# Two edits in a two-layer attention trunk: one gate projection moved in the fill order, and a bias moved from TensorE to GpSimd and VectorE

## The chip, the cores and the metric

One Trainium2 chip, one core. The metric is the device time of one execution in microseconds (us). TensorE (PE) multiplies matrices, VectorE (DVE), ScalarE (ACT) and GpSimd (POOL) do the rest, SyncE (SP) issues the DMAs. A matmul shows twice in the trace, as a weight load (PEld) and as the pass of the moving columns (PE).

## The reference, cut to what matters

Two layers on 1024 tokens of width 1024, in float32. Layer 1 holds an attention that keeps the 256 best keys of each query (DSA, "a") and a sliding-window attention ("b"); layer 2 holds a compressed, selected and windowed attention (NSA, "c") and a latent attention ("d"). Each output is multiplied by silu of a gate projection ("z").

```python
y = rms_norm(x, norm_g) @ w_in              # layer 1: qa ka va qi ki wi za qb kb vb zb
score = sum_h wi * relu(qi @ ki.T)          # index scores
idx = top_k(score, 256)                     # a search of 32 steps here, giving a mask
oa = attention(qa, ka, va, masked by idx)
ob = sliding_window_attention(qb, kb, vb)
x = x + concat(oa * silu(za), ob * silu(zb)) @ w_out

# layer 2, one part of it: the compression of keys (n=0) and values (n=1)
def nsa_compress(z, pe, w1, w2):            # z: 63 overlapping blocks of 32 tokens
    flat = (blocks + pe).reshape(..., 32 * 64)
    return silu(flat @ w1) @ w2             # w1: 2048 x 128
```

`flat @ w1` is worked out as `blocks @ w1 + pe @ w1`. The second term is the position bias, 128 numbers for each n.

## The kernel before, in words

Tokens are cut into 8 tiles of 128. All projections of a layer are cut into chunks of up to 280 columns. For a chunk, `w_quarter` loads the weights (line 472), splits them into a high part on ACT (line 476) and a low part on POOL (line 477); `fill_gen` then makes 24 matmuls for each token tile (lines 520 to 522, into one of two `pp` banks of PSUM), and the chunk's `post` empties the bank.

* A query chunk (`qa0`, `qa1`, `qb0`, ...) empties through `pair_in`: two ACT copies for each tile (lines 452 and 454, the second into the one `sq` buffer). Two tiles make a pair, which goes through `head_chain` (POOL and DVE) to a transpose (line 392) and to one of three `qs` buffers (lines 396 and 399). The chain holds one of four `nz` buffers until the transpose.
* A gate chunk (`z0`, `z1`, `z2`) empties through `gate_post`: one ACT tanh (line 610), one DVE product (line 611), one DMA out. `z2` has 270 columns, `qa0` and `qa1` have 256 each.

`FAO` is the order in which the chunks of layer 1 are issued as fill beside the other work, by planned costs. A query chunk is held back (`q_gate`) while all three `qs` buffers are in use. The search for the 256 best keys (`topk`) runs beside this: a step counts on ACT (line 904, three token tiles) and on DVE (line 908, three tiles), compares (line 919) and moves the candidate (line 921). When the second half of the search ends, lines 960 to 966 build the masks, one for each of the token tiles 2 to 7; each mask uses one of the three `pt` buffers, which the attention of "b" and "a" also uses for its scores (lines 680 and 683). The blocks of "a" from tile 2 on wait for their masks.

The framework under the kernel orders the instructions of each engine: what is issued earlier in the program has priority, what is ready earlier by its own estimate may go in front. On the chip each engine then runs its own list in that order.

In layer 2, `compress` is posted when the chunk `kc` ends, and runs in small steps between the fill's matmuls of the chunk `kw`. For n = 0 and then for n = 1 it loads `pe` and `w2`, makes the bias by 16 matmuls of one column each (line 1265), multiplies the blocks by the same 16 weight tiles (line 1276), and goes on with tanh, `w2` and the key or value form. The first-layer compression weights `w1` (1 MB for each n) lie in slots of a five-slot pool; the trace calls them `w`. The load of the second `w1` (line 1224) is issued when a slot of that pool comes free.

Of the kernel before, what the change touches and what calls it, by code (L numbers as in the profile page):

```python
# [10 lines left out]
F32 = mybir.dt.float32  # L11
# [7 lines left out]
OP = mybir.AluOpType  # L19
AX = mybir.AxisListType  # L20
PSUM = bass.MemoryType.PSUM

P = 128
# [29 lines left out]
BR = 0.8  # L53
AR = 1.2

FAO = 'ki qi kb qb0 z0 z1 qb1 ka qa0 z2 qa1'
FOO = 'ks kc kw qc0 zc0 zc1 cq qc1 zd0 zd1 ck'
SR = 0.6
GDA = [2, 3, 7], [4, 5, 6]
# [11 lines left out]
PTB = 3  # L71
# [113 lines left out]
def trunk(ctx: ExitStack, tc: tile.TileContext, A, out):  # L185
    nc = tc.nc
    V, S, G, T = nc.vector, nc.scalar, nc.gpsimd, nc.tensor
# [4 lines left out]
    wk = ctx.enter_context(tc.tile_pool(name="wk", bufs=2))  # L192
# [25 lines left out]
    half = cst.tile([P, 16], F32, name="half")  # L218
# [140 lines left out]
    def tps():  # L359
        return psT.tile([P, 4, P], F32, name="psT")  # L360
# [679 lines left out]
    z0 = zlo + 206  # L1040
    z1 = z0 + 274
# [34 lines left out]
    def seq(*gens):  # L1076
        for g in gens:
# [3 lines left out]
                  qa0=c_qa[0], qa1=c_qa[1])  # L1081
    FA = fill_gen([chunks[n] for n in FAO.split()])
    L.pump(FA, ("qi", 2))
# [4 lines left out]
    for c in tk:  # L1088
        m += c
        L.tick()  # L1090
        while f < TR * m and c is not None:
            c = next(FA)
# [161 lines left out]
    def compress():  # L1254
        for n in range(2):
            w1 = B["w1"][n]
            zT = B["zT"][n]
            pe = cp.tile([P, 16], F32, name="pe")
            nc.sync.dma_start(pe, A["c_cmp_pe"][0, n].rearrange("(a b) d -> (b d) a", b=2))
            w2 = cp.tile([P, 64], F32, name="w2")  # L1260
            nc.sync.dma_start(w2, A["c_cmp_w2"][0, n])
            yield from L.take_in("psT", PTC)
            ph = tps().rearrange("p a n -> p (a n)")
            for a in range(16):
                T.matmul(ph[:, 0:1], w1[:, a], pe[:, a:a + 1], start=a == 0, stop=a == 15)
            bias = cp.tile([P, 2], F32, name="bias", bufs=2)
            V.tensor_copy(bias[:, 0:1], ph[:, 0:1])
            L.give("psT")
            V.tensor_scalar(bias[:, 1:2], bias[:, 0:1], 0.5, None, op0=OP.mult)
            yield  # L1270
# [4 lines left out]
            for a in range(16):  # L1275
                T.matmul(p2[:, :, 0:NCMP], w1[:, a], zT[:, :, 2 * a:2 * a + 16 * (NCMP - 1) + 1:16],
                         start=a == 0, stop=a == 15)
# [196 lines left out]
    def cchunk(*a, **k):  # L1474
        return chunk(*a, src="x1T", **{"tiles": AO[1], **k})

    c_kc = cchunk(wcd, CD["kc"], CD["ks"], kc_post, pre=kc_pre,
                 post_all=lambda: L.post(compress()))
    c_ks = cchunk(wcd, CD["ks"], CD["kw"], ksq, pre=ksp)
    c_kw = cchunk(wcd, CD["kw"], CD["zc"], kw_post, pre=kwp, post_all=kw_all)  # L1480
# [387 lines left out]
```

## Time and profile before

| what | value |
|---|---|
| median of 3 runs | 1495.83 us (1494.69 to 1501.79) |
| profiled execution, its own time | 1506.33 us |
| its span, first to last instruction | 1504.5 us |
| mean granted TensorE clock in it | 0.944 |
| PE busy in the span | 1331.0 us (88%) |
| DVE, ACT, POOL busy | 1004.0, 939.7, 908.6 us |

The profiled execution is one run, with the profiler on; it lies 10.5 us above the median. Durations are read from it, differences are carried over to the median.

### The profile page before, as it was taken

To read this page: it belongs to the slowest core of one execution; us is meant where nothing else is said; L and a number is where in the kernel's file an instruction comes from. 1 tells how busy PE (TensorE), PEld (TensorE's weight loads), DVE (VectorE), ACT (ScalarE), POOL (GpSimd) and SP (SyncE) were. 2 spreads that over 40 slices of the span, in tenths; PEclk is the share of its full clock that TensorE was granted. 3 is DMA by queue.
4 is the path that set the end of the run, shared out by engine and by line. 5 is a ranking of instruction groups with operands and counts; after the bars stand their busy time and mean duration, and the time that the engine had idled before them with its cause. 6 is when DMAs were issued, how large, how long until landed. Compare 5 with 4: busy or idle time off the path is not lost. (4 is left out here: it accounts for less than half of the span.)

```text
span 1504.5 us, 33785 instructions
## 1 busy us (share of the span) xinstructions
PE 1331.0 (88%) x12132; PEld 1221.2 (81%) x12132; DVE 1004.0 (67%) x2788; ACT 939.7 (62%) x2683; POOL 908.6 (60%) x1196
## 2 busy tenths in 40 slices
PE   5998899888248999999999998899998868889998
PEld 5998888788247788999999997699996757778887
DVE  5397887787887966244225757756668889986552
ACT  5354588877658866144424677866768869866531
POOL 6798648896467486227349353365244799875440
PEclk9999999898659999999999999999999879999999
DMA  6311264322041244132311253312334414334442
GB/s 205 91 32 31 68 134 92 81 49 69 12 109 59 83 108 131 44 120 70 75 33 53 75 106 76 64 46 62 78 61 71 117 56 98 82 86 102 128 128 79
DMA packets 208936, 122.81 MB, mean 82 GB/s; under 512 B 141696, under 2 KB 193664, under 8 KB 208768
## 3 DMA queue, kind: packets, MB, share of 16 engines
q1 hardware_dynamic: 208768, 120.65, 32.0%
q8 instruction: 95, 1.56, 0.4%
q14 instruction: 73, 0.60, 0.1%
HBM read 67.65 MB, written 23.07 MB: 60 GB/s over the span
## 5 line engine op out<-in xcount | busy, mean ns | idle before, releaser
L520 PE MATMUL pp<-whi,Rh 128*128 128x256 f32 (+4 forms) x1648 | 483.2, 294 | 22.7 <-ACT sq L454 6.6
L521 PE MATMUL pp<-wlo,Rh 128*128 128x256 f32 (+4 forms) x1648 | 477.6, 290 | 1.1 <-POOL wlo L477 1.1
L522 PE MATMUL pp<-whi,Rl 128*128 128x256 f32 (+4 forms) x1648 | 478.2, 290 | 0.0
L520 PEld LDWEIGHTS pp<-whi,Rh 128*128 128x128 f32 x1648 | 319.3, 194 | 28.4 <-ACT sq L454 7.7
L521 PEld LDWEIGHTS pp<-wlo,Rh 128*128 128x128 f32 x1648 | 319.4, 194 | 3.1 <-POOL wlo L477 1.5
L522 PEld LDWEIGHTS pp<-whi,Rl 128*128 128x128 f32 x1648 | 319.4, 194 | 1.1
L689 ACT ACTIVATE pt<-pt,nm 128x256 f32<-128x256 f32 (+8 forms) x384 | 244.9, 640 | 5.5
L477 POOL TENSOR_TENSOR wlo<-wraw,whi 128x256 fp32r<-128x256 f32 (+4 forms) x208 | 163.5, 795 | 129.2 <-ACT whi L476 123.0
L711 POOL TENSOR_TENSOR hl<-pt,hl 128x512 f16<-128x512 f32 x114 | 136.9, 1203 | 110.1 <-ACT hl L710 83.6
L476 ACT ACTIVATE whi<-wraw 128x256 fp32r<-128x256 f32 (+4 forms) x208 | 83.2, 416 | 135.6 <-DMA wraw<-in_cd_w_in 48.2
L730 PE MATMUL psT<-identf,pt 128*128 128x128 f32 x800 | 144.7, 286 | 12.4 <-ACT pt L689 6.0
L733 ACT ACTIVATE hp<-psT 128x512 f16<-128x512 f32 (+3 forms) x241 | 109.0, 462 | 59.9 <-PE psT L730 55.5
L683 DVE CUSTOM_DVE_ANT_0 pt<-psS,mk 128x512 f32<-128x512 f32 (+4 forms) x208 | 107.0, 522 | 47.9 <-PE psS L680 37.1
L734 DVE TENSOR_TENSOR hp<-psT,hp 128x512 f16<-128x512 f32 (+3 forms) x241 | 123.3, 521 | 23.1 <-ACT hp L733 21.7
L303 POOL TENSOR_TENSOR rs_y<-rs_v,half 128x8 f32<-128x8 f32 (+3 forms) x102 | 122.5, 1203 | 3.9
L730 PEld LDWEIGHTS psT<-identf,pt 128*128 128x128 f32 x800 | 95.5, 144 | 26.2 <-ACT pt L689 13.7
L660 PEld LDWEIGHTS <-hp 128*128 128x128 f16 x800 | 73.4, 98 | 26.0 <-ACT hp L733 7.6
L687 ACT ACTIVATE nm<-nm 128x1 f32<-128x1 f32 (+2 forms) x208 | 42.0, 203 | 83.6 <-DVE nm L683 82.4
L663 PEld LDWEIGHTS <-hp 128*128 128x128 f16 x800 | 72.1, 98 | 23.8 <-DVE hp L734 14.7
L661 PEld LDWEIGHTS <-hp 128*128 128x128 f16 x800 | 73.7, 99 | 2.7 <-issue 1.8
L710 ACT ACTIVATE hl<-pt 128x512 f16<-128x512 f32 x114 | 71.0, 628 | 7.6 <-DMA ht<-hl 4.9
L689 ACT ACTIVATION_READ_ACCUMULATOR pt<-pt,nm 128x1 f32 x384 | 73.5, 191 | 0.0
(317 smaller groups left out, 3641.8 us busy)
## 6 DMA issues: line engine op xcount, KB each, us to landing
wraw<-in_cd_w_in SPq DMA_DIRECT2D x72, 128.0 KB, 2.1
wraw<-in_ab_w_in SPq DMA_DIRECT2D x56, 128.0 KB, 2.5
xs<-in_x SPq DMA_DIRECT2D x8, 512.0 KB, 6.0
od<-mx SPq DMA_DIRECT2D x32, 128.0 KB, 1.9
wraw<-in_ab_w_out SPq DMA_DIRECT2D x32, 128.0 KB, 2.2
x<-in_x SPq DMA_DIRECT2D x8, 512.0 KB, 4.7
mo<-od SPq DMA_DIRECT2D x16, 256.0 KB, 3.0
nz<-zdr SPq DMA_DIRECT2D x16, 256.0 KB, 3.0
```

The costliest lines, as they stand in the source:

```text
L303: G.tensor_tensor(y, v, half[:w, :n], OP.pow)
L476: S.activation(hi[:, :o], raw[:, :o], AF.Copy)
L477: G.tensor_tensor(lo[:, :o], raw[:, :o], hi[:, :o].bitcast(F32), OP.subtract)
L520: T.matmul(ps, xh, hi[:, :n], start=q == 0 and k == 0, stop=False)
L521: T.matmul(ps, xh, lo[:, :n], start=False, stop=False)
L522: T.matmul(ps, xl, hi[:, :n], start=False, stop=q == 3 and k == 1)
L683: V.tensor_tensor_reduce(pt[:, j * nk + c:j * nk + c + w], ps[:, at:at + w], mask(c, w), -1.0, first, op0=OP.add, op1=OP.min, accum_out=low)
L689: S.activation(pt[:, j * nk:(j + 1) * nk], pt[:, j * nk:(j + 1) * nk], AF.Exp, scale=-1.0, bias=nm[:, h:h + 1], accum_out=sm[:, h:h + 1])
L711: (V if way[-1] == "d" else G).tensor_tensor(hl[:, w:], pt[:, o:o + w], hl[:, :w], OP.subtract)
L730: T.transpose(pT[:, a], pt[:, o:o + P], identf)
L733: S.activation(ph, pT[:, :n], AF.Copy)
L734: V.tensor_tensor(pl, pT[:, :n], ph, OP.subtract)
```

## The change

`FAO` issues the gate chunk `z2` directly behind `ka`, in front of the query chunk `qa0`; before, it came between `qa0` and `qa1`. And `compress` makes its position bias in another way: POOL multiplies the 16 weight tiles by `pe` (two products of 128 x 1024), DVE sums each product over its 8 tiles (two reductions to 128 x 128), and PE sums over the partitions by two matmuls with a column of the constant `half` (-0.5); the factor -2 goes into the copy out of PSUM. Two more steps (`yield`) stand in the generator. The product takes a `pt` buffer, the sums an `mx` buffer.

```diff
-FAO = 'ki qi kb qb0 z0 z1 qb1 ka qa0 z2 qa1'
+FAO = 'ki qi kb qb0 z0 z1 qb1 ka z2 qa0 qa1'
@@ compress()
             w2 = cp.tile([P, 64], F32, name="w2")
             nc.sync.dma_start(w2, A["c_cmp_w2"][0, n])
+
+            u = wk.tile([P, 256], F32, name="pesum", tag="mx", bufs=3)
+            for a in range(0, 16, 8):
+                t = wk.tile([P, 1024], F32, name="pt", bufs=PTB).rearrange("p (a c) -> p a c", a=8)
+                G.tensor_tensor(t, w1[:, a:a + 8], pe[:, a:a + 8, None].to_broadcast([P, 8, P]), OP.mult)
+                V.tensor_reduce(u[:, 16 * a:16 * a + P], t.rearrange("p a c -> p c a"), AX.X, OP.add)
+                yield
             yield from L.take_in("psT", PTC)
             ph = tps().rearrange("p a n -> p (a n)")
-            for a in range(16):
-                T.matmul(ph[:, 0:1], w1[:, a], pe[:, a:a + 1], start=a == 0, stop=a == 15)
+            for a in range(2):
+                T.matmul(ph[:, 0:1], u[:, a * P:(a + 1) * P], half[:, 0:1], start=a == 0, stop=a == 1)
             bias = cp.tile([P, 2], F32, name="bias", bufs=2)
-            V.tensor_copy(bias[:, 0:1], ph[:, 0:1])
+            V.tensor_scalar(bias[:, 0:1], ph[:, 0:1], -2.0, None, op0=OP.mult)
             L.give("psT")
```

## Rows read from the trace of the kernel before

**Rows 1.** Windows: us of the stretch, then busy us of each engine, clock, DMA

```profile
450.00:600.00 150.00, 137.68 (x1608) 122.08 (x1607) 109.70 (x320) 115.70 (x302) 101.89 (x128) 0.98 0.31 93
600.00:916.00 316.00, 311.31 (x2737) 305.98 (x2736) 139.88 (x412) 143.73 (x428) 148.96 (x213) 0.97 0.27 73
```

**Rows 2.** Waits of PE between 600 and 916: the longest in total, times, longest

```profile
PE pp L520 <- DVE x L1160: 1.7, 2, 1.4
```

**Rows 3.** Timeline of PE: first matmuls of qa0, z2 and qa1, and the gap

```profile
291.49 0.58 PE L520 MATMUL pp<-whi,Rh 128*128 128x256 f32 x1 [3.75 <-DVE vla L603]
...
329.06 0.37 PE L520 MATMUL pp<-whi,Rh 128*128 128x270 f32 x1
...
360.56 0.28 PE L520 MATMUL pp<-whi,Rh 128*128 128x256 f32 x1
...
404.31 0.79 PE L680 MATMUL psS<-kb,qs 128*128 128x256 f32 x2 [22.42 <-DVE nm L683]
```

**Rows 4.** By line or tile: count, min/median/max ns, first and last start

```profile
L921 DVE SCALAR_TENSOR_TENSOR cand<-inc,less x15: 166/167/899, 318.4 to 391.9; 128x6 f32<-128x6 f32 x15
...
L921 DVE SCALAR_TENSOR_TENSOR cand<-inc,less x5: 167/167/596, 376.4 to 391.9; 128x6 f32<-128x6 f32 x5
...
L960 ACT ACTIVATE sel<-hi,K x4: 624/772/926, 301.4 to 414.3; 128x384 bf16<-128x384 int16 x1, 128x512 bf16<-128x512 int16 x1, 128x640 bf16<-128x640 int16 x1, 128x768 bf16<-128x768 int16 x1
...
L680 PEld LDWEIGHTS psS<-ka,qs x44: 186/192/338, 432.6 to 469.7; 128*128 128x128 f32 x44
```

**Rows 5.** Groups of ACT between 312.7 and 395.6: busy us, mean ns, idle before

```profile
L610 ACT ACTIVATE zst<-pp 128x270 f32<-128x270 f32 x8 | 3.1, 385 | 2.6 <-PE pp L522 2.4
L454 ACT ACTIVATE sq<-pp 128x256 f32<-128x256 f32 x8 | 3.0, 374 | 0.0
L452 ACT ACTIVATE nz<-pp 128x256 f32<-128x256 f32 x8 | 2.9, 368 | 0.7 <-PE pp L522 0.7
```

**Rows 6.** Timeline of PE's weight loads around the two biases

```profile
740.38 0.48 PEld L1239 LDWEIGHTS psT<-identf,ydup 128*128 128x128 f32 x4
740.84 4.35 PEld L1265 LDWEIGHTS psT<-pe,w 128*128 128x128 f32 x32
...
745.07 5.24 PEld L1276 LDWEIGHTS psT<-zT,w 128*128 128x128 f32 x24
750.20 0.32 PEld L520 LDWEIGHTS pp<-whi,Rh 128*128 128x128 f32 x1
...
751.11 1.61 PEld L1276 LDWEIGHTS psT<-zT,w 128*128 128x128 f32 x8
...
765.36 4.91 PEld L1265 LDWEIGHTS psT<-pe,w 128*128 128x128 f32 x32
770.14 0.33 PEld L522 LDWEIGHTS pp<-whi,Rl 128*128 128x128 f32 x1
...
771.46 5.14 PEld L1276 LDWEIGHTS psT<-zT,w 128*128 128x128 f32 x24
```

**Rows 7.** Windows around the biases, columns as in rows 1

```profile
745.00:750.00 5.00, 5.00 (x25) 5.00 (x25) 0.31 (x2) 0.72 (x2) 1.42 (x2) 0.50 0.30 47
...
760.00:765.00 5.00, 5.00 (x41) 4.94 (x39) 2.00 (x5) 1.09 (x5) 4.69 (x11) 1.00 0.02 5
...
770.00:775.00 5.00, 5.00 (x24) 4.97 (x25) 1.42 (x5) 1.17 (x5) 2.09 (x3) 0.56 0.00 0
```

**Rows 8.** Groups by shape, POOL and DVE: nearest to the new operations

```profile
L374 POOL TENSOR_TENSOR nz<-nz,rs_y 128x512 f32<-128x512 f32 x24 | 25.7, 1072 | 0.6
L1512 POOL TENSOR_TENSOR Rl<-wraw,Rh 128x512 fp32r<-128x512 f32 x16 | 22.0, 1375 | 0.3 <-ACT Rh L1511 0.3
L595 DVE TENSOR_REDUCE vs_m<-pt 128x1 f32<-128x1024 f32 x5 | 6.1, 1218 | 3.7 <-DMA pt<-in_cd_w_in 2.0 <-DMA pt<-in_ab_w_in 1.7
```

**Rows 9.** Compression weights: issues on SP (first and last start), and the landing

```profile
L1224 SPq DMA_DIRECT2D w<-in_c_cmp_w x2: 718/772/826, 717.3 to 753.2; - x2
...
DMA to landing us min/median/max: 2.2/4.2/6.6
```

## The prediction

> **What bounds the kernel now.** I read the page first: PE is busy 88% of the span, no other engine over 67%. Then windows along the whole span, to see where that average hides something. Between 600 and 916 us PE is busy 311 of 316 us [rows 1], and the waits of PE in that stretch add up to little, the longest group to 1.7 us [rows 2]: here PE alone sets the end, so a microsecond of PE work that goes is a microsecond won, and what follows starts earlier by as much. Both biases of the compression lie in that stretch. Between 450 and 600 us (attention "a") PE is busy 138 of 150 us and stands idle for 12.3 [rows 1].
>
> The other half of the change lies in front of that. In the timeline of PE, `qa0` starts at 291.49, `z2` at 329.06, `qa1` at 360.56, and at 404.31 a product of "b" begins after 22.4 us in which PE did nothing [rows 3]. The reader should see that PE waits there for no projection: the wait is on DVE, and the search for the best keys runs there, its candidate moved for the last but one time at 391.9 [rows 4]. The masks copied in from 301.4 on hold `pt` buffers until the search ends [rows 4], and the last blocks of "b" need those. So the end of the search starts the rest of layer 1; the first product of "a" follows at 432.6 [rows 4].
>
> **The moved chunk.** Nothing is added or removed: 8 tiles of 24 matmuls of `z2`, their 8 ACT tanhs, 8 DVE products and 8 DMAs out, and the weight loads of the chunk on SP with their splits on ACT and POOL, change places with those of `qa0`. On PE, the two chunks take the place from 291.49 to 360.56 in either order, and behind `qa1` lie 22.4 idle us as cover [rows 3]; without them a longer sequence would cost its own length. On SP and POOL the 8 gate stores and 8 + 8 weight loads and splits trade places; what waits for a gate store is read only when "a" is mixed, after 432.6. What is late next is `qa0`: its queries come about 31.5 us later (329.06 to 360.56 is the length of `z2`), and the first product that needs them has stood ready for 141 us less its chain of copies and transposes (291.49 to 432.6) [rows 3, 4]. That is cover enough.
>
> The search itself is what this move can touch. Late, when little else runs, a step takes (391.9 - 376.4) / 4 = 3.9 us; over all of this half it takes (391.9 - 318.4) / 14 = 5.25 [rows 4], so some 19 us of it are disturbance by other work on ACT and DVE. A tile of a query chunk costs ACT 368 + 374 = 742 ns, one of the gate 385 [rows 5]. Now 8 query tiles and 8 gate tiles empty during the search's second half: 5.9 + 3.1 = 9.0 us. After the move I expect the gate's first 5 or so in front of it and 4 more query tiles inside it: 12 x 0.742 + 3 x 0.385 = 10.1. So the search ends some 1 us later at most, if every ACT microsecond counts; 0 if the tiles lie in its idle time. I take 0.5.
>
> **The bias.** The 16 matmuls (32 weight loads) of n = 0 occupy PE from 740.84 to 745.07, 4.23 us, those of n = 1 from 765.36 to 770.14, 4.78 us [rows 6]: 9.0 us. Two matmuls of the same kind come back for each, 4 loads of 32: 9.0 / 8 = 1.1 us. Net 7.9 us less on PE.
>
> Behind each bias the clock is low: granted 0.50 from 745 to 750 and 0.56 from 770 to 775, and 1.00 from 760 to 765, between the two [rows 7]; 0.5 is 1.2 of 2.4 GHz. What ran before that were matmuls of one column. If it now stays up, what ran at half clock after the biases gets faster, but that is mostly the 16 matmuls on the blocks, and these don't follow the clock: 24 loads in 5.13 us at half (0.214 each), 8 in 1.61 at full (0.201) [rows 6]. They can win 0.5 us together at most, and I leave that out. What does follow it: six projection loads from 750.20 to 751.11, 0.91 us where six of the stretch's mean (2736 in 316 us, 0.116 each [rows 1]) take 0.70: 0.2 us; and from 770.14 to 771.46 two loads and four transposes, 1.32 us where four transposes take 0.46 at full clock (740.38 to 740.84) and two mean loads 0.23: 0.6 us [rows 6]. Gain 0.8 us. The Trainium skill ("TensorE: Matmul & The Clock Gate", section Terms) prices the halved time at the time itself x (1 - K/N), here one half. By that, the 4.9 us after 745.07 and some 4.3 us after 770.14 would give back 4.6 us, and the sum of the bias would be 12.5 us instead of 8.7. The rows on the blocks' matmuls speak against it, so it stands among the rivals.
>
> What comes in: four POOL products of 128 x 1024. The trace has none; twice the shortest row of 512 columns is 2.1 us, twice the longest 2.75 [rows 8]; with a broadcast operand it is like the first, on float32 weights like the second; I take 2.6. And four DVE reductions of 128 x 1024 to 128 x 128, read with a stride: one to a single column takes 1.22 us [rows 8], which I take, with twice that, 2.4, as the upper end for the stride. Together 10.4 us of POOL and 5 to 10 us of DVE, beside engines that are busy 149 and 140 of 316 us there [rows 1]; only their latency could cost. For n = 0 the weights are issued at 717.3 and landed within 6.6 us, by 724; two products and the last reduction then end by 730.4 (732 at the upper ends), 9 to 10 us ahead of 740.84 [rows 6, 8, 9]. For n = 1 there is no such cover: the second weights are issued at 753.2, right behind the last block matmuls of n = 0 (751.11 + 1.61), which free their slot, and land up to 6.6 us later. With PE 3.7 us ahead by then (4.23 less 0.55) that is 756; plus 6.4 us is 762.5, and the bias's place on PE, moved up, is 761.7 [rows 6, 9]. POOL was 4.69 of 5 us busy from 760 to 765 [rows 7], so the products can stand behind other work. The 280-column tiles of `kw` can be issued in front of the two matmuls, so I take 0 for this wait of 0.8 us; its upper end is the POOL work of that window, 4.7 us, plus 1.2 for a slower reduction: 6 us. Queued behind a waiting reduction on DVE are the copies that empty the `pp` banks of `kw`, and PE waits for those; that is in the 6.
>
> **Sum.** -7.9 - 0.8 + 0.5 = -8.2 us. On the profiled execution, 1506.3 us, that is 1498.1; it lies 10.5 us over the median of the runs, and the difference carried to the median gives 1495.83 - 8.2 = 1487.6.
>
> **Rivals.** Half a per cent, 7.5 us, is about what a measurement of this kernel can tell from no change; the line lies at 1488.4.
> 1. *All of it, as summed:* 1487.6, own range 1485 to 1490. Chance 0.44.
> 2. *The clock is worth more:* the halved time counts by its half, the block matmuls too. 1495.8 - 12.5 + 0.5 = 1483.8, and down to 1480 if the search also ends earlier. For it: the clock row. Against: the two spacings. Chance 0.13. By the skill's rule this would be the likeliest.
> 3. *PE waits for the sums of n = 1:* up to 6 us given back, 1490 to 1494. For it: the late landing and the busy POOL. Chance 0.17. Here also belongs that the change doesn't do what it says, PE waiting as long as it saved.
> 4. *The search ends later by 3 to 5 us,* since the pairs' chains and copies now all fall into its second half, on both its engines: 1491 to 1493. For it: 19 us of disturbance now. Against: the same work in total. Chance 0.14.
> 5. *Slower:* without `z2` between them, `qa0` and `qa1` ask for `nz` buffers one right after the other. `qa0` has four pairs and there are four buffers; if none of its pairs has been transposed when `qa1` starts, PE stops there until "a" frees queries. Six tiles of `qa1` that now end before 382 (21.3 us from 360.56) then run between 450 and 600, and 12.3 idle us there [rows 1] can hide part or none: +9 to +21, less 8.2: 1497 to 1509, over the line of +0.5% if less than about 6 us are hidden. It decides from the first pair of `qa1` on. Against: the chains would have the 22 us of the gap to catch up. Chance 0.12.
>
> **How the numbers follow.** Likeliest: 1487.6. Rivals 1 and 2 give faster (1 only in some three of four cases, its range crosses the line): 0.33 + 0.13 = 0.46. The rest of 1, with 3, 4 and a third of 5, is the same: 0.11 + 0.17 + 0.14 + 0.04 = 0.46. Slower 0.08. For 8 in 10 the range runs from 1481, inside rival 2, to 1497, where rival 5 begins; the likeliest alone has 1485 to 1490.
>
> **What would show it.** On the bias: the two groups of 32 loads gone, 4 loads each in their place, granted clock 1.00 from 740 to 775 (if it still falls, the block matmuls are its cause), block matmuls still 0.20 to 0.21 us apart, no idle time of PE in front of the two matmuls of n = 1. POOL products near 2.6 us, reductions between 1.2 and 2.4. On the moved chunk: 270-column matmuls first, `qa1` ending near 382, the last move of the candidate within 1 us of 391.9, the product of "b" at 404 to 405. A stretch from 600 to 916 that shrinks by about 8.7 us and a front that ends where it did would be this sum; a front that moves by more than 3 us either way would make it wrong, since the order of each engine's list is settled anew and can shift other work.

## The result and the profile after

The changed kernel takes 1514.36 us in the median of 4 runs (1508.59 to 1517.9) against 1496.16 for the kernel before, now of 4 runs as well: ratio 1.0111 [1.0091, 1.0131]. Run again beside the first experiments it gave 1.0082 [1.0055, 1.0109]. It is slower by about 1%, where the prediction had 0.55% faster; the time lies outside its range.

The two profiled executions hide this. The one of after is the fastest of its four runs (1508.59), the one of before lies 10.5 us over its median, so they differ by 2 us. A pair of profiles shows here what each instruction does, not what the change costs. For that the ratios below are used, and a second profile of the kernel before (1501.97 us, span 1500.2, experiment `e0`).

Windows of after, the stretches of [rows 1, 7], columns as there:

```profile
450.00:600.00 150.00, 134.35 (x1551) 118.46 (x1550) 106.41 (x306) 110.65 (x284) 100.66 (x126) 0.97 0.29 89
600.00:916.00 316.00, 307.82 (x2733) 299.80 (x2730) 149.51 (x427) 144.42 (x437) 158.73 (x219) 0.99 0.28 75
745.00:750.00 5.00, 5.00 (x29) 4.84 (x28) 0.93 (x4) 0.77 (x3) 0.73 (x1) 1.00 0.19 52
760.00:765.00 5.00, 4.72 (x36) 4.73 (x37) 3.70 (x6) 1.80 (x9) 5.00 (x9) 1.00 0.02 5
770.00:775.00 5.00, 5.00 (x30) 4.85 (x29) 1.07 (x4) 1.40 (x4) 4.52 (x9) 1.00 0.23 66
```

The clock stays at 1.00 behind both biases, where it had been 0.50 and 0.56. But PE is busy 307.8 of 316 us in the stretch where it had been busy 311.3, and 134.4 of 150 in attention "a" (137.7 before): idle time has come in at both places that the change touches (the second stretch is shown more closely below).

Instructions by line, after (count, min/median/max ns, first and last start), in answer to [rows 4, 6, 8]:

```profile
L1267 DVE TENSOR_REDUCE pesum<-pt x4: 1965/1977/2025, 723.2 to 759.9; 128x128 f32<-128x1024 f32 x4
...
L1272 PEld LDWEIGHTS psT<-half,pesum x8: 190/192/192, 738.3 to 770.8; 128*128 128x128 f32 x8
...
L921 DVE SCALAR_TENSOR_TENSOR cand<-inc,less x15: 166/167/1139, 319.2 to 386.0; 128x6 f32<-128x6 f32 x15
```

The group of the four products on POOL, after (busy us, mean ns of one | idle before):

```profile
L1266 POOL TENSOR_TENSOR pt<-w,pe 128x1024 f32<-128x1024 f32 x4 | 7.5, 1900 | 12.0 <-DMA w<-in_c_cmp_w 12.0
```

A product takes 1.90 us, a reduction 1.98. The search's second half is shorter than before: from the first to the last move of its candidate 66.8 us (319.2 to 386.0), against 73.5 in [rows 4].

Timeline of POOL in after, around the second sum (start, us, instruction, idle before and what ended it):

```profile
755.41 3.75 POOL L1266 TENSOR_TENSOR pt<-w,pe 128x1024 f32<-128x1024 f32 x2 [9.39 <-DMA w<-in_c_cmp_w]
...
768.57 1.28 POOL L413 TENSOR_TENSOR ydup<-nz,rp_t 128x512 f32<-128x512 f32 x1
```

That of DVE:

```profile
757.35 1.98 DVE L1267 TENSOR_REDUCE pesum<-pt 128x128 f32<-128x1024 f32 x1 [2.42 <-POOL pt L1266]
...
759.92 1.97 DVE L1267 TENSOR_REDUCE pesum<-pt 128x128 f32<-128x1024 f32 x1
```

And that of PE:

```profile
760.28 0.40 PE L520 MATMUL pp<-whi,Rh 128*128 128x280 f32 x1 [1.47 <-ACT gat L1348]
...
770.13 0.60 PE L420 MATMUL psT<-identf,ydup 128*128 128x128 f32 x4
770.57 0.50 PE L1272 MATMUL psT<-half,pesum 128*128 128x1 f32 x4
770.93 7.10 PE L1283 MATMUL psT<-zT,w 128*128 128x126 f32 x32
...
780.06 0.24 PE L1298 MATMUL psT<-w,hid 128*64 128x64 f32 x1 [1.59 <-issue]
...
781.22 0.27 PE L567 MATMUL psT<-identf,vs_m 128*1 128x128 f32 x1 [0.70 <-DVE vs_m L1329]
```

The sums are ready at 761.89 (759.92 + 1.97). The two matmuls that use them start at 770.57, 8.7 us later, with no idle time in front of them: they stand in PE's list behind four transposes (L420) of a `kw` pair, whose last product on POOL starts at 768.57. PE's idle time stands elsewhere: 1.47 us for a `pp` bank at 760.28, 1.59 in front of the product with `hid`, 0.70 in front of `vs_m`.

### The profile page after: what moved, and what is told of

The parts are those of the page before. It is cut to its first block, busy times and chain, and to the rows that moved or that the text cites. A ratio compares the mean times of both kernels' runs of the same rounds, so it can differ in the third digit from the quotient of the medians.

```text
span 1506.5 us, 33680 instructions
## 1 busy us (share of the span) xinstructions
PE 1323.6 (88%) x12076; PEld 1208.8 (80%) x12076; DVE 1008.2 (67%) x2792; ACT 934.8 (62%) x2683; POOL 914.8 (61%) x1200
## 5 line engine op out<-in xcount | busy, mean ns | idle before, releaser
L520 PEld LDWEIGHTS pp<-whi,Rh 128*128 128x128 f32 x1648 | 315.6, 192 | 24.1 <-ACT sq L454 5.9
L521 PEld LDWEIGHTS pp<-wlo,Rh 128*128 128x128 f32 x1648 | 315.5, 192 | 3.2 <-POOL wlo L477 1.6
L522 PEld LDWEIGHTS pp<-whi,Rl 128*128 128x128 f32 x1648 | 315.5, 191 | 1.1
```

What stands on the lines that cost most here:

```text
L520: T.matmul(ps, xh, hi[:, :n], start=q == 0 and k == 0, stop=False)
L521: T.matmul(ps, xh, lo[:, :n], start=False, stop=False)
L522: T.matmul(ps, xl, hi[:, :n], start=False, stop=q == 3 and k == 1)
```

## The experiments

Theory A (the prediction's own steps): the time is lost at the second sum, or at the moved chunk. Theory B: the work is as cheap as summed, and what costs is the order of the lists, which the framework settles anew from the edit to the end of the kernel. Ratios are to the kernel before, run beside each on the same chip, with 95% intervals in brackets. The recorded expectations letter their theories anew for each group; the order of the lists is "O" there.

**The two halves apart.** `e0` is the kernel before again. `e1` has only the first hunk of the diff, `e2` only the second, `e3` is the changed kernel.

The whole edit of `e1`, against before:

```diff
-FAO = 'ki qi kb qb0 z0 z1 qb1 ka qa0 z2 qa1'
+FAO = 'ki qi kb qb0 z0 z1 qb1 ka z2 qa0 qa1'
```

That of `e2`, against after:

```diff
-FAO = 'ki qi kb qb0 z0 z1 qb1 ka z2 qa0 qa1'
+FAO = 'ki qi kb qb0 z0 z1 qb1 ka qa0 z2 qa1'
```

> The kernel before, unchanged, for a second profile of it. The profiled execution of before lies 10.5 us above the median of its runs, that of after 5.8 us below its own, so the two profiles differ by 2 us where the medians differ by 18. If that is one chance wait, this profile has a span near 1494 and the stage that is shorter by some 10 us in it is where the profile of before was unlucky. If the spread of before lies all over the span, no stage differs by more than 3 us.

> Only the moved chunk; the bias stays on PE. Theory A (the moved gate chunk costs: the chunks of queries a, back to back, take z2 from the place where it filled PE, and every list behind is settled anew): about 1510, ratio 1.010. Theory B (the bias on POOL and DVE costs): 1496, ratio 1.000. Theory C (only the pair costs, by a list that comes out badly with both edits): 1496 and the bias alone at or under 1496.

> Only the bias on POOL and DVE; the chunks stay in the old order. Theory A (the moved chunk costs): 1487 to 1490, the 8 us that leave PE are won. Theory B (the products on POOL and the reductions on DVE make PE wait around 750 to 800, or the lists behind are settled worse): about 1510, ratio 1.010. Theory C (only the pair costs): 1488 to 1496.

> The changed kernel on the same chip as the halves: ratio 1.009 to 1.013 as before, about 1512. If the ratio differs by chip, it comes out below 1.005 or above 1.016.

Measured: `e1` 1501.86 us, 1.0030 [1.0012, 1.0049]; `e2` 1508.91 us, 1.0071 [1.0048, 1.0093]; `e3` 1.0082. The halves add up (1.01), and each loses alone, so none of the ranges of a single cause holds. `e0` differs from the first profile of before by 4.4 us, in small pieces over the whole span: so much is chance in a single profile.

The cost of `e1` shows in attention "a". Timeline of PE in `e1`:

```profile
530.57 0.20 PE L660 MATMUL po<-vha,hp 128*128 128x64 f16 x1 [2.60 <-POOL hp L738]
...
542.09 0.20 PE L663 MATMUL po<-vha,hp 128*128 128x64 f16 x1 [3.77 <-POOL hp L739]
```

That of `e0`, at the same product:

```profile
530.55 0.23 PE L660 MATMUL po<-vha,hp 128*128 128x64 f16 x1 [2.74 <-POOL hp L738]
```

The first wait is in both; the second, 3.8 us for a product of POOL, is 0.4 us in `e0` and 2.6 in after. "a" starts no later in `e1` (its first product with the keys at 429.6, 431.4 in `e0`), but from there to its last such product it takes 162.4 us, against 156.1.

**Order or work.** Here the order of each engine's list is held. Behind the whole program every instruction gets an edge from the one that stands in front of it in another kernel's list; the edge sets the order of issue and adds no wait on the chip.

```diff
+    for k, steps in order.items():
+        at = [j + s for j, s in enumerate(steps)]
+        for a, b in zip(at, at[1:]):
+            tc.add_manual_dep(rows[k][b], rows[k][a].name, info, reason="order")
```

`e4`: the work of before, and everything issued behind the compression in the order of `e2`. `e5`: the work of `e2`, and behind the compression the order of before. `e6`: the bias left out and set to 0, the order of before everywhere. `e7`: before with the two extra steps of the generator and no other change.

`e6`, against before, then `e7` (of `e6` the loop above and its list are left out here):

```diff
-            yield from L.take_in("psT", PTC)
-            ph = tps().rearrange("p a n -> p (a n)")
-            for a in range(16):
-                T.matmul(ph[:, 0:1], w1[:, a], pe[:, a:a + 1], start=a == 0, stop=a == 15)
             bias = cp.tile([P, 2], F32, name="bias", bufs=2)
-            V.tensor_copy(bias[:, 0:1], ph[:, 0:1])
-            L.give("psT")
-            V.tensor_scalar(bias[:, 1:2], bias[:, 0:1], 0.5, None, op0=OP.mult)
+            V.memset(bias, 0.0)
```

```diff
+            yield
+            yield
             yield from L.take_in("psT", PTC)
```

> The kernel before, its bias on PE as it was, but each engine issues everything that is emitted behind the compression in the order that it has in the kernel with the new bias (issue order alone, no wait added). Theory O (the new bias costs little where it stands; the lists behind it, settled anew, cost): 1505 to 1512, as slow as the new bias alone or slower, since the 8 us of PE are still spent. Theory D (the products and reductions themselves make PE wait between 750 and 830 and that cost is carried to the end): 1496 to 1500.

> The mirror image: the bias on POOL and DVE, and each engine issues everything that is emitted behind the compression in the order of the kernel before. Theory O: 1486 to 1492, the 8 us of PE less some 4 us in which PE waits in the stretch of the compression. Theory D: 1505 to 1510, as the new bias alone.

> The bias of the compression is left out (set to 0, so the compressed keys and values are computed without it) and nothing stands in its place; all lists keep the order of the kernel before. The most that taking the bias off PE can give. If a microsecond of PE that goes in this stretch is a microsecond won, as the prediction's sum has it: 1488 to 1490 (9.0 us less on PE, and a little of the clock). If the gain is given back further on whatever the order is, because the granted clock falls there instead: 1494 to 1499.

> The kernel before with its work unchanged; the generator of the compression only pauses twice more in front of each bias, as it does in the changed kernel, so the lists behind it are settled anew. Theory O: a time that differs from before by more than 3 us, either way, since an edit without any work re-orders the lists as well. Theory D: 1497 to 1499, no difference.

Measured: `e4` 1506.87 us, 1.0066 [1.0049, 1.0083]; `e5` 1501.67, 1.0039 [1.0021, 1.0057]; `e6` 1493.01, 0.9981 [0.9965, 0.9997]; `e7` 1500.31, 1.0017 [1.0001, 1.0034]. With none of the new work, the order costs 0.66%, though `e4`'s profile has a 4.2 us wait for a `pp` bank, ended at 791, that `e0` has not; `e11` below is free of it. Some of the loss stays when the order is taken away (`e5`, between its two ranges), so B alone doesn't do. `e6` gains 0.19%, about 3 us, though 9.0 us of PE work are gone and nothing stands in their place. `e7` fits neither of its theories: two more steps without any new work cost 0.17% [0.01, 0.34], and 0.7 us of PE's idle time in front of `vs_m` is there too, so this part of after's idle time comes with the steps and not with the sums.

**One sum at a time, and the chunk with its old order.** `e8` makes the first sum (n = 0) in the new way and the second by 16 matmuls, `e9` the other way round, both with the order of before behind the compression. `e10` has the moved chunk and the bias of before, and from about 510 us on the order of before.

`e8` (`e9` has `n == 1` in its first line):

```diff
+            if n == 0:
...
+                for a in range(2):
+                    T.matmul(ph[:, 0:1], u[:, a * P:(a + 1) * P], half[:, 0:1], start=a == 0, stop=a == 1)
+            else:
...
+                for a in range(16):
+                    T.matmul(ph[:, 0:1], w1[:, a], pe[:, a:a + 1], start=a == 0, stop=a == 15)
```

> Only the first of the two biases (n = 0) is summed on POOL and DVE, the second stays on PE; everything emitted behind the compression in the order of before. The prediction's reading (the sums of n = 0 are done 9 to 10 us before PE wants them, so their 4.2 us less 0.55 are all won): 1494 to 1495 beside 1498. If the new work costs by its load on POOL and DVE wherever it lies: about 1499 to 1500, half of the 4 us that both together cost in the old order.

> Only the second bias (n = 1) on POOL and DVE, the first stays on PE; the order of before behind the compression. The prediction's rival 3 (the weights of n = 1 land late, PE and the copies queued behind the reductions wait): this one carries the whole loss, 1501 to 1504. If load alone costs: 1499 to 1500 as the other half. If the loss is one of the order in the stretch of the compression itself: both halves near 1498.

> Only the moved chunk, and from the middle of attention a on (about 510 us) every engine issues in the order of before. Theory O for the front (the search and the first products come 1.6 us earlier, and the re-settled list of a gives back more in its waits for POOL at 530 to 545): 1495 to 1498, the 3.6 us of the moved chunk gone. If the queries of a cost by themselves (they come later, or in a worse order for the first half of a): 1500 to 1502, as with its own order.

Measured: `e8` 1498.14 us, 0.9973 [0.9954, 0.9993]; `e9` 1502.58, 1.0012 [0.9996, 1.0027]; `e10` 1502.15, 1.0011 [0.9994, 1.0028]. The first sum wins 4 us, the second gives back what it takes off PE, and by its median something more. In `e10` the second wait of "a" is gone from the trace, "a" takes 156.4 us again, and no loss is left that can be told from zero. But the ratio's interval overlaps that of `e1`, and `e10` differs in front of "a" as well: its search's second half takes 70.2 us, not the 66.2 of `e1`, and its first product of "a" comes at 435.7. So the order of its list is shown to be where "a" loses its 6 us; that this is all of the chunk's loss is likely, not settled.

Windows from 735 to 805, where both biases lie, of `e0`:

```profile
735.00:805.00 70.00, 70.00 (x508) 68.91 (x506) 20.78 (x58) 22.41 (x77) 38.01 (x60) 0.90 0.19 47
```

Of after:

```profile
735.00:805.00 70.00, 66.03 (x475) 63.98 (x474) 26.36 (x65) 24.16 (x81) 45.48 (x68) 0.98 0.17 45
```

Of `e8`:

```profile
735.00:805.00 70.00, 70.00 (x506) 68.64 (x505) 21.87 (x59) 24.00 (x81) 41.48 (x66) 0.95 0.17 47
```

Of `e9`:

```profile
735.00:805.00 70.00, 65.75 (x468) 64.11 (x467) 25.19 (x61) 22.36 (x77) 42.59 (x64) 0.93 0.19 45
```

Before, PE has no idle microsecond there. With the first sum alone it still has none. After has 4, and `e9` 4.25: the idle time comes with the second sum.

**Which part of the order, and must a new order lose?** `e11`: the work of before; only from the first product of "c" on the order of `e2`, the compression left to the framework. `e15`: the same for "d" and the output alone. `e12`: `e8`'s work, no list. `e13`: `e6`'s work (no bias), no list.

The list of `e4` begins at instruction 10950 of the program. `e11`, then `e15`, against `e4` (the list itself, left out here, is shortened with `FROM`), and what `e12` takes from `e8` and `e13` from `e6` (`_in_order` is the function that holds the loop above):

```diff
-FROM = 10950
+FROM = 11177
```

```diff
-FROM = 10950
+FROM = 18300
```

```diff
     with tile.TileContext(nc, **_TC) as tc:
         trunk(tc, aps, o[0])
-        _in_order(tc)
```

> The kernel before, its bias on PE; each engine issues what is emitted from the first product of attention c on in the order that it has with the new bias, and the 140 instructions between the compression and that product are left free, so that the wait of 4.2 us for a gate at 778 of the earlier exchange is not forced. If the order of the long part behind (c and d) costs by itself: 1502 to 1506. If the cost of the exchanged order was that one wait: 1497 to 1500.

> The same work as in the run with the first sum alone (n = 0 on POOL and DVE, n = 1 on PE, ratio 0.9973 in the order of before), but with the lists as they settle by themselves. If it is the one order of the changed kernel that is bad: 0.997 again. If any order settled anew loses against that of before: 1.000 to 1.004.

> The bias left out (set to 0) with the lists as they settle by themselves; in the order of before the same work had a ratio of 0.9981. If only the changed kernel's order is bad: 0.997 to 0.999. If any order settled anew loses: 1.001 to 1.005, slower than before with 9 us less work on PE.

> The kernel before, its bias on PE; only what is emitted from the last products of c on (all of d and the output) is issued in the order of the kernel with the new bias. With c in that order as well the ratio was 1.0059. If c and d share the cost as the two traces share it (4.6 us before 960, 2 to 3 us of PE standing still between 1184 and 1350): 1.001 to 1.003. If c carries all: 1.000. If d carries all: 1.005 to 1.006.

Measured: `e11` 1508.99 us, 1.0059 [1.0038, 1.0080]; `e15` 1500.28, 1.0021 [1.0006, 1.0036]; `e12` 1496.33, 0.9982 [0.9966, 0.9998]; `e13` 1491.56, 0.9963 [0.9947, 0.9979]. `e11` does the work of before in another order and is 0.6% slower; "d" holds about a third of that, and by difference "c" the rest. But `e12` and `e13` run in orders of their own and lose nothing by it that can be told from zero (`e8` and `e6` do the same work in the old order), and the new order of `e7` costs 0.17%: it is this order that is bad, not every new one.

Windows of `e0` over parts of "c" and "d":

```profile
805.00:1000.00 195.00, 185.05 (x1960) 169.21 (x1959) 129.81 (x464) 137.56 (x436) 90.12 (x115) 0.99 0.34 76
1230.00:1350.00 120.00, 101.67 (x945) 86.67 (x944) 105.86 (x277) 95.33 (x261) 105.65 (x123) 0.94 0.37 89
```

Of `e11`:

```profile
805.00:1000.00 195.00, 183.54 (x1908) 165.84 (x1907) 127.94 (x464) 134.71 (x430) 86.49 (x109) 0.98 0.34 74
1230.00:1350.00 120.00, 99.42 (x911) 83.02 (x911) 103.35 (x278) 96.51 (x270) 108.12 (x125) 0.94 0.37 87
```

PE does 1.5 and 2.3 us less in the same stretches, at nearly the same clock, in some 50 and 30 fewer matmuls. After has the second of these marks too (99.08 from 1230 to 1350). The loss has no single wait: the largest that is new between 805 and 1000 is 1.6 us (PE for `hp` of DVE).

**Both sums once more.** `e14`: both sums, from the first product of "c" on the order of before. `e16`: as `e14`, with the products on DVE. `e17`: `e16` without the list.

`e14` against `e5` (the list left out again), then `e16` and `e17`, each against `e14` but for the list:

```diff
-FROM = 10950
+FROM = 11163
```

```diff
-                G.tensor_tensor(t, w1[:, a:a + 8], pe[:, a:a + 8, None].to_broadcast([P, 8, P]), OP.mult)
+                V.tensor_tensor(t, w1[:, a:a + 8], pe[:, a:a + 8, None].to_broadcast([P, 8, P]), OP.mult)
```

> Both biases on POOL and DVE; the order of before is laid on only from the first product of attention c on, the stretch of the compression is left to settle. If the 0.39% of both sums in the old order is the price of the new work (the wait of n = 1): 1.003 to 1.005 again. If it came from the list that was forced through the stretch of the compression, where the two halves gave -0.27% and +0.12%: 0.998 to 1.001.

> Both sums, but the four products run on DVE instead of POOL; the order of before from the first product of attention c on, as in the run of both sums with the late order (ratio 1.0044, PE still for 4.0 us between 735 and 805, its bias matmuls of n = 1 at 767.5 though the sums were ready at 758.8). If the loss is made by the products standing on POOL in front of the key chain whose transposes PE takes before that bias (last ydup of it at 766.84): the bias comes 3 to 6 us earlier, PE stands still for less than 1.5 us, and the ratio is 0.996 to 1.000. If it is the load on DVE, the landing of the weights or the order itself: 1.003 to 1.006.

> The same with the lists as they settle by themselves, a third order behind the compression. With POOL as the cause and an order no worse than that of before: 0.996 to 1.000. If orders settled anew with both sums lose as that of the changed kernel does: 1.004 to 1.008.

Measured: `e14` 1504.59 us, 1.0044 [1.0028, 1.0059]; `e16` 1505.46, 1.0048 [1.0027, 1.0069]; `e17` 1502.8, 1.0033 [1.0012, 1.0055]. Taking the products off POOL doesn't take the idle time away: PE waits longer. But `e16` puts them on DVE, so it doesn't tell what part POOL has in after. `e17` lies between its two ranges. Waits of PE in `e16` from 735 to 805 (us, times, longest):

```profile
PE pp L520 <- ACT gat L1348: 6.3, 1, 6.3
```

Its timeline of DVE there:

```profile
755.08 2.36 DVE L1266 TENSOR_TENSOR pt<-w,pe 128x1024 f32<-128x1024 f32 x2 [5.30 <-DMA w<-in_c_cmp_w]
...
757.55 1.86 DVE L1267 TENSOR_REDUCE pesum<-pt 128x128 f32<-128x1024 f32 x1
...
759.48 1.75 DVE L1267 TENSOR_REDUCE pesum<-pt 128x128 f32<-128x1024 f32 x1
761.15 0.33 DVE L603 SCALAR_TENSOR_TENSOR vlw<-pp,vs_e,vhw 128x128 f16<-128x128 f32 x1
```

Products and reductions hold DVE from 755.08 to 761.23, and the operation that empties the `pp` bank (L603) stands behind them. So what PE waits for at the second sum is its banks, behind whatever DVE is given to do; in after, with the products on POOL, that is 1.47 us, and POOL's chain of the `kw` pair is late besides.

## Why the prediction was wrong

The forecast was that of the work alone. Three of its steps failed: the order of the lists had no price and costs 0.6%; the wait for the second sum was put at 0, and the idle time around it takes back all that this sum takes off PE; and a microsecond off PE was not a microsecond won, since even with no bias at all less than the 8.7 us of the sum were gained. The moved chunk, priced at 0.5 us, costs 0.30%, most likely by its list in "a".

**The sizes of the operations** were near: a product 1.90 us (2.6 expected, 2.1 to 2.75 the bounds), a reduction 1.98 (1.22 taken, 2.4 the upper end), four loads of 0.19 for each bias. The sums came when expected, since the one error took back the other.

**"A microsecond of PE work that goes is a microsecond won"** did not hold. `e6` and `e13` leave both biases out, 9.0 us of PE work, and put nothing in their place. By the sum's own terms (9.0, and 0.8 for the clock) that is 9.8 us. Measured are 0.19% [0.03, 0.35] in the old order and 0.37% [0.21, 0.53] in its own: about 3 and 5.5 us, at most 7.9. So the 8.2 us forecast were out of reach even if the new work and its order had cost nothing. The one profile of `e6`, its fastest run, gains 7.0 us between 735 and 804 against `e0`; where the runs lose the rest is not shown.

**The first sum** did what the working said, within the interval: 4.23 less 0.55 us is 3.7, and `e8` shows 4.0 (0.27% [0.07, 0.46]).

**The clock** is at 1.00 in all the windows that the prediction named. That it is worth more than 0.8 us (the second rival) isn't borne out: the 7.0 us of `e6` are less than the 9.0 of the matmuls themselves. The blocks' matmuls, which fill most of the halved time, keep their pace. Timeline of PE's weight loads in after, at 1.00:

```profile
741.80 6.76 PEld L1283 LDWEIGHTS psT<-zT,w 128*128 128x128 f32 x32
```

That is 0.211 us each, where it was 0.214 at 0.50. The Trainium skill ("TensorE: Matmul & The Clock Gate", section Terms), with half of the halved time given back, would have made the gain of `e6` about 13.6 us (9.0 + 4.6, an estimate from its rule); the run does not agree with it.

**"I take 0 for this wait"** failed too. The sums came at 761.89, as the working had it (762.5), and PE didn't wait for them by name. But the two matmuls stood 8.7 us further down PE's list, and 4 us of PE were lost around them, at the bank and at the small products behind. The second sum was to win 4.2 us net and costs 0.12% [-0.04, 0.27] (`e9`). The third rival held the mechanism, the banks behind DVE's reductions included; the value taken was wrong.

**The moved chunk:** the cover for `qa0` held, and the fifth rival did not occur: "a" starts no later (first product at 428.0 in after, 428.6 in `e3`, 429.6 in `e1`; in the sixteen profiles with the chunk in its old place at 428.2 to 434.0). The price of the search had the wrong sign: its second half, expected up to 1 us longer, takes 66.2 to 66.8 us in these three and 69.6 to 73.5 in those sixteen. That the tiles of ACT add up to its length is what failed there; why it is shorter was not looked into. The loss lies inside "a", which takes 162.1 to 162.8 us from its first to its last product with the keys, against 155.2 to 157.8. The largest wait in it, 3.8 us for POOL in `e1`, is one that the prediction did not look for; it had followed the chunk only as far as the front.

**The order of the lists** is the step whose absence decided. The prediction's last sentence names it as what would make it wrong, and gives it no price and no chance. It costs about 0.6% by itself, 9 us, with the work of before (`e11`: 0.59% [0.38, 0.80]). That is the size of the whole forecast, with the other sign. A rival "the lists are settled anew and lose" would have had its ground where the front tells how the framework orders each engine.

**The sum.** The chunk's 0.30% and the bias's 0.71% make the 1%. The 0.71% does not split cleanly: both sums with the old order cost 0.39 to 0.44% (`e5`, `e14`), the order alone 0.59%, together more than they cost jointly.

**What stays open** is why both sums together lose 0.4% when each alone, in the old order, gives -0.27% and +0.12%. Up to 805 us the halves add up in the profiles. Behind that, `e14`'s PE is busy 182.4 of 195 us from 805 to 1000 where `e0` has 185.1, `e8` 185.9 and `e9` 185.6, and near 1165 the clock falls (below). Set instruction for instruction against `e0`, `e5` and `e14` lose 3.7 and 4.9 us between 805 and 1000 and 5.7 and 3.9 between 1155 and 1185, while `e8` and `e9` stay within 0.5 us in both. At both places PE waits for a late transfer of the kind that the last section reads, for 2.4 us in the first one. That explains a part; how often it comes in the runs that were not profiled isn't known.

The best version seen is the first sum alone: 0.9973 with the old order, 0.9982 with its own. It beats the kernel before by some 0.2%.

## What to carry to other kernels

Where a framework settles the order of issue, an edit has a second price that no row of the trace shows: here it was 0.6% in one order and nothing in others, so give it a chance and a range of its own, and measure the edit with the old order held before judging the work. Leave the work out altogether as well, once: that gives the most that the edit can win, and here it was less than the forecast. Moving work off the bounding engine won where its inputs were long there (the first sum) and lost where they came late (the second): what counts is not only whether the result is in time, but what stands behind the new work on its own engine, above all the copies that empty the bounding engine's banks. One profile of each kernel can lie 10 us from its median; compare medians first, then read.

## What the hardware showed beyond that

**A DMA that takes 1.85 us longer is followed by a delay of 7.** `e5` and `e0` run the same order here. The chain of waits of `e0` (start, us, what):

```profile
1160.75 3.03 DMA ht<-hl
```

Its windows:

```profile
1160.00:1170.00 10.00, 9.16 (x106) 8.76 (x103) 9.43 (x36) 7.06 (x30) 7.73 (x17) 1.00 0.43 82
1170.00:1180.00 10.00, 8.24 (x84) 6.18 (x83) 8.10 (x35) 8.16 (x33) 5.67 (x12) 1.00 0.17 55
```

The chain of `e5`:

```profile
1160.93 4.88 DMA ht<-hl
```

Its timeline of PE behind that:

```profile
1167.57 0.20 PE L660 MATMUL po<-vhw,hp 128*128 128x64 f16 x1 [0.91 <-ACT hp L733]
...
1168.67 1.01 PE L730 MATMUL psT<-identf,pt 128*128 128x128 f32 x4 [0.87 <-DVE hp L734]
```

And its windows:

```profile
1160.00:1170.00 10.00, 7.99 (x91) 7.25 (x87) 7.66 (x31) 6.52 (x29) 7.53 (x15) 0.94 0.40 77
1170.00:1180.00 10.00, 10.00 (x74) 9.73 (x74) 4.31 (x18) 3.33 (x18) 2.65 (x8) 0.50 0.03 5
```

The transfer takes 4.88 us, not 3.03; PE idles about 2 us within 10, the granted clock goes to 0.50 (1.2 of 2.4 GHz), and the projection's matmuls then follow each other at 0.21 us in place of 0.11. The delay against `e0`, 0.2 us in front of the transfer, is 2 at 1167 and 7 at 1175; the spans end 6.1 apart (1506.3 and 1500.2). This is in the profiles of `e2`, `e3`, `e5`, `e14` and `e16`, which all make both sums, and in none of a kernel with one sum or none; but after and `e17` make both and don't show it.

The traces also show what that transfer met. PE's instructions come in by packets of 16 KB on a DMA queue of their own (q8): 95 in a run, with about 256 of PE's instructions from one to the next. In `e5` such a packet starts at 1163.78, 2.85 us after the transfer; of the transfer's 16 parts 15 have landed by 1164.22, the last at 1165.80. In all five profiles with the delay the packet starts 2.6 to 2.85 us after, and the last part comes 1.5 us or more behind the others. In `e0` it starts at 1160.01, ahead of the transfer. Over all twenty profiles, a transfer of `ht` that is issued without delay takes 3.0 to 3.7 us where the packet starts up to 1.5 us ahead of it (153 cases) and 3.8 to 4.8 where it starts 1.25 to 2.4 us behind (75 of 76); from 2.4 to 2.9 us 63 of 149 are over 4.2 and 85 under 3.4, those of after and `e17` here (2.47 and 2.56) among the latter. Both sums take 112 instructions out of PE's list of 24264, and so its packets fall elsewhere. No run moves the packets alone, and a late transfer need not cost much: `e9` has one of 4.21 us at 1160.38, at a clock of 1.00. Of `e5`'s 12 runs five take 1505 to 1508.5 us, the profiled one among them, and seven 1498 to 1502, so the delay may come in some of its executions only.

**A strided reduction** of 128 x 1024 to 128 x 128 takes 1.98 us on DVE, against 1.22 to a single column [rows 8], and the product with a broadcast operand about 1.2 us on DVE (2.36 for two) against 1.90 on POOL.
